# A new plan for the pieces of work behind an expert's twelve weight blocks

## The chip, the cores and the metric

The kernel runs on one core of a Trainium2 chip. The metric is the device time of one execution in microseconds (us), read as the median of several runs. A measurement of this kernel can tell a difference of about 0.2% (some 4 us) from no change.

## The reference, cut to what matters

One layer: a token mixer (which the change does not touch), then a mixture of experts over 1024 tokens of width 1024, a residual add and a last norm. The part that matters, per token block of an expert:

```python
logits = (xt @ w_router + b_router)
top_vals, top_idx = lax.top_k(logits, 4)            # 4 of 32 experts
weights = jax.nn.softmax(top_vals, axis=-1)
...
def expert_block(args):
    xblk, e = args
    gu = xblk @ w_gu[e] + b_gu[e]                    # 1024 -> 2048
    gate, up = jnp.split(gu, 2, axis=-1)
    gate = jnp.minimum(gate, 7.0); up = jnp.clip(up, -7.0, 7.0)
    act = (up + 1.0) * gate * jax.nn.sigmoid(1.702 * gate)
    return act @ w_down[e] + b_down[e]               # 1024 -> 1024
...
y = zeros.at[buf_tok].add(yb * buf_w[:, None])       # rows back to their tokens
```

## The kernel before, in words

**Experts and blocks.** The experts are sorted by how many tokens they have and run in a written-out order, `HHHLLH`, then twelve times `LH`, then `LL` (line 1344). Every expert takes 128 tokens in a main group; a heavy one (H) has one further group of 32 tokens, called the remainder, and the first expert has two. An expert's weights come in twelve blocks of 1 MB, each [128, 2048] in fp32: eight of `w_gu` and four of `w_down`. The loop at line 1770 runs one iteration per expert e: the eight `w_gu` blocks of expert e (`gu_chunk`, blocks 0 to 7), then the four `w_down` blocks of expert e-1 (`dn_chunk`, blocks 8 to 11). With them the activation of expert e (`act`) is put out at block 8, and the weighted rows of e-1 are scattered at the end (`finish_e`). The first iteration has eight blocks only.

**A block.** The matrix products are made exact by splitting each fp32 operand into a high and a low part: ScalarE (ACT) copies the block into the high part, VectorE (DVE) subtracts it to get the low part (`split`, lines 130 to 134), and TensorE (PE) then runs twelve matmuls of 512 columns for the block. The split blocks stand in three buffers `hl`, so ACT can split a block as soon as PE has used the one three places before. For a remainder PE runs further matmuls (`pR`) straight from the fp32 blocks, after blocks 3, 7 and 11. The weights lie in eight slots and are loaded up to five blocks ahead, in order, on the queue of SP.

**The pieces.** Between two blocks `extras(k)` puts out small pieces of work that the next experts need; `plan(e)` (line 1736) is the hand-written list of which piece stands behind which block k. They are:
- `prep_a(e, 0)` and `prep_a(e, 1)`: PE transposes half of the activated rows of expert e into PSUM (`pps`, four transposes), ACT copies the high part, DVE subtracts the low part. `prep_a(e, 2)` does the remainder rows (`ppr`, two transposes): a copy by ACT and no VectorE part.
- `prep_x(e, 0)`, `(e, 1)`, `(e, 2)`: the same for the gathered input rows.
- `prep_sel(e)`: a one-hot table by DVE. `prep_route(e)`: PE multiplies it with a table of indices and weights (`pq`), DVE forms row indices from the result, and GpSimd (POOL) starts the indirect DMAs that gather the rows (`xg`, and `xq` for a remainder).
- In the first two iterations also `bias_rows` (bias tables, four of them), `route_weights` (a transpose `px`, a copy `wT` by ACT, a matmul `pyw`, then five steps that alternate between ACT and DVE), `weigh` (the weights of the first two experts), and `route_counts` and `route_rows` (tables for an overflow path).

**What sets the order.** All of these pieces write one and the same PSUM bank, the single buffer of `ptr` with the tag "t". PE's instructions keep the order of the program (`T.strict`), so PE stands still if a piece comes up while the bank still holds the piece before, that is until ACT and DVE have read it. On ACT and DVE the instructions go through one queue each, in an order that the scheduler of the framework fixes at build time, mostly by which is ready first. POOL's queue holds the gathers and the scatter-adds into `acc` of `finish_e`, where the scatter of remainder rows (`yq`) waits until the scatter of the main rows (`y`) has landed.

Of the kernel before, what the change touches and what calls it, by code (L numbers as in the profile page):

```python
# [9 lines left out]
F32 = mybir.dt.float32  # L10
# [9 lines left out]
P = 128  # L20
# [6 lines left out]
NE = 32  # L27
# [25 lines left out]
def tile_hybrid_layer(ctx: ExitStack, tc: tile.TileContext, x, c, ctx_in, c_ctx, w_ada, b_ada, norm_mix_w,  # L53
# [35 lines left out]
    def pool(name, **kw):  # L89
        return tc.tile_pool(name=name, bufs=kw.pop("bufs", 1), reuse_waits="tile", **kw)  # L90
# [89 lines left out]
    tp = inp.enter_context(pool("tp", bufs=2))  # L180
# [287 lines left out]
    at = [kp.tile([P, 2, 2, P], F32, name=f"at{d}") for d in range(2)]  # L468
# [356 lines left out]
    pb = inp.enter_context(pool("pb"))  # L825
# [74 lines left out]
    lg = rp.tile([P, NT, NE], F32, name="lg")  # L900
# [285 lines left out]
    pdn = mps.enter_context(pool("pdn", space=PSUM))  # L1186
    prm = mps.enter_context(pool("prm", space=PSUM))
    ptr = mps.enter_context(pool("ptr", space=PSUM))
    tp = ms.enter_context(pool("tp3"))
# [33 lines left out]
    for i, v in enumerate((0, 5)):  # L1223
        S.activation(info[:, :, :, v], tcol[:, i, :, None].to_broadcast([P, NT, NE]), AF.Copy)
        S.activation(info[:, :, :, v + 1], pcols[:, i:i + 1, None].to_broadcast([P, NT, NE]), AF.Copy)

    def route_weights():

        flat = lg.rearrange("p t e -> p (t e)")
        S.activation(lgn, lg, AF.Copy)  # L1230
        G.tensor_tensor(bdg, bdg, g2b[0:96], op=ALU.mult)
        px = ptr.tile([P, 2, P], F32, name="px", tag="t")
        for h in range(2):
            T.transpose(px[:, h], flat[:, h * P:(h + 1) * P], ident)
        wT = tp.tile([P, 2, P], F32, name="wT")
        S.activation(wT, px, AF.Copy)
        py = ptr.tile([P, 2, P], F32, name="pyw", tag="t")
        for h in range(2):
            T.matmul(py[:, h], wT[:, h], pbd.rearrange("p j e -> p (j e)"), start=True, stop=True)
        V.tensor_copy(flat, py.rearrange("p h r -> p (h r)"))  # L1240
        eq = tp.tile([P, NT, NE], F32, name="eq")
        S.activation(info[:, :, :, 2], lg, AF.Copy)
        V.tensor_tensor(eq, lg, info[:, :, :, 2], op=ALU.subtract)
        S.activation(info[:, :, :, 3], eq, AF.Copy)
        V.tensor_tensor(eq, eq, info[:, :, :, 3], op=ALU.subtract)
        S.activation(info[:, :, :, 4], eq, AF.Copy)
        for j in range(4):
            S.activation(g2r[32 * j:32 * j + 32], g2b[32 * j:32 * j + 32, 256 * j:256 * j + 256], AF.Copy)

    B = {}  # L1250

    def route_blocks():

        erb = B["erb"] = tp.tile([NE, 2 * NE + 1], F32, name="erb")
        V.tensor_copy(erb[:, 0:NE], pe_[:NE, 0:NE])

    def route_counts():
# [6 lines left out]
        for j in range(7):  # L1264
            dst = nb if j == 0 else tmp1
            V.tensor_scalar(dst, over, float(P * j), None, op0=ALU.is_gt)
            if j:
                V.tensor_tensor(nb, nb, tmp1, op=ALU.add)
        nbb = B["nbb"] = tp.tile([NE, 2, MAXBLK], F32, name="nbb")
        V.tensor_copy(nbb[:, 0], nb.to_broadcast([NE, MAXBLK]))  # L1270
        V.tensor_copy(nbb[:, 1], capc.to_broadcast([NE, MAXBLK]))

    def route_rows():

        nbb, erb = B["nbb"], B["erb"]
        pb = ptr.tile([P, 3, NE], F32, name="pblk", tag="t")
# [45 lines left out]
    def bias_perm():  # L1322
        perm = ap.tile([P, 2 * D], BF16, name="perm", tag="y")[:, 0:1536].rearrange(
            "p (a q n j i) -> p a q n j i", a=3, q=4, n=4, j=8)
        V.memset(perm, 0.0)
        for i in range(3):
            V.tensor_copy(perm[:, i, :, :, :, i], pbd.rearrange("p n (q j) -> p q n j", q=4))
        return perm

    def bias_rows(perm, q):  # L1330
        pb = ptr.tile([P, 512], F32, name="pbq", tag="t")
        for i in range(3):
            T.matmul(pb, perm[:, i, q].rearrange("p n j i -> p (n j i)"), bt[:, i], start=(i == 0), stop=(i == 2))
        S.activation(bq[:, q], pb, AF.Copy)
# [26 lines left out]
    def route_main(i, pq, main):  # L1361

        r, sel = order[i], R["sel", i]
        for t in range(NT):
            T.matmul(pq[:, 0, main], sel[:, t, 0:P], info[:, t, r, main], start=(t == 0), stop=(t == NT - 1))

    def route_rem(i, pq, rem):

        r, sel = order[i], R["sel", i]
        for g in range(nrem[i]):  # L1370
            for t in range(NT):
                for j in range(4):
                    T.matmul(pq[32 * j:32 * j + 32, 1 + g, rem], sel[:, t, P + CAPR * g:P + CAPR * (g + 1)],
                             info[:, t, r, rem], start=(t == 0), stop=(t == NT - 1))
# [27 lines left out]
    def slot_weights(i, pq):  # L1402
        n = 1 + nrem[i]
        wc = xp.tile([P, 3], F32, name="wc", tag="wc", bufs=4)
        V.tensor_reduce(wc[:, :n], pq[:, :n, 2:5], axis=mybir.AxisListType.X, op=ALU.add)  # L1405
        R["wc", i] = wc
# [85 lines left out]
            HL[key] = hl  # L1492
            pos_split[0] += 1

    GU, DN = {}, {}

    def gu_start(e):
        g = pgu.tile([P, 4, 512], F32, name="pG", tag="g")
        rs = []
        if nrem[e]:  # L1500
            rs.append(prm.tile([P, 512], F32, name="pR", tag="r"))
        if nrem[e] > 1:
            rs.append(pdn.tile([P, 2, 512], F32, name="pR1", tag="d")[:, 0])
        GU[e] = (g, rs)

    def gu_bias(e):
# [198 lines left out]
    with tc.high_priority():  # L1705
        for i in range(2):
            if i == 0:
                prep_sel(0, (slice(0, P), slice(P, P + CAPR * nrem[0])))
            pq = ptr.tile([P, 3, 8], F32, name="pq", tag="t")
# [4 lines left out]
            pq = pdn.tile([P, 3, 8], F32, name="pqr", tag="d")  # L1714
# [11 lines left out]
            prep_x(0, p_)  # L1726
    perm = bias_perm()

    def weigh(i):
        pq = ptr.tile([P, 3, 8], F32, name="pq", tag="t")  # L1730
        route_main(i, pq, slice(2, 5))
        route_rem(i, pq, slice(2, 5))
        slot_weights(i, pq)


    def plan(e):
        todo = {}

        def at(k, f, *a):
            todo.setdefault(k, []).append((f, a))  # L1740
        if e == 0:
            for k, q in ((0, 0), (2, 2), (4, 1)):
                at(k, bias_rows, perm, q)
            at(1, route_weights)
            at(3, prep_x, 1, 2)
            at(5, weigh, 0)
            at(5, weigh, 1)
            at(6, prep_x, 1, 0)
            at(7, prep_x, 1, 1)
            at(7, prep_sel, 2)  # L1750
            return todo
        if e == NE:
            return todo
        for k, p in ((0, 0), (2, 1), (4, 2)):
            at(k, prep_a, e - 1, p)
        if e + 1 < NE:
            for k, p in ((5, 0), (7, 1), (9, 2)):
                at(k, prep_x, e + 1, p)
        if e == 1:
            at(1, prep_route, 2)  # L1760
            at(3, route_counts)
            at(6, route_rows)
            at(11, bias_rows, perm, 3)
        if e + 2 < NE:
            at(8, prep_sel, e + 2)
            at(10, prep_route, e + 2)
        return todo

    T.strict = True
    for e in range(nexp + 1):  # L1770
        todo = plan(e)

        def extras(k):
            for f, a in todo.pop(k, ()):
                f(*a)
        if e < nexp:
            gu_start(e)
            for k in range(KT):
                advance()
                gu_chunk(e, k)  # L1780
                extras(k)
# [28 lines left out]
    with ExitStack() as st:  # L1810
# [3 lines left out]
        pdn = st.enter_context(tc.tile_pool(name="pdn2", bufs=1, space=PSUM, reuse_waits="tile"))  # L1814
        ptr = st.enter_context(tc.tile_pool(name="ptr2", bufs=1, space=PSUM, reuse_waits="tile"))
        again = nc.values_load(nblk1[0:1, 1:2], min_val=0, max_val=1)  # L1816
        with tc.For_i(0, again, 1):
# [5 lines left out]
            with tc.For_i(0, nblk, 1) as ib:  # L1823
# [27 lines left out]
                pq = ptr.tile([P, 8], F32, name="opq", tag="t")  # L1851
                for t in range(NT):
                    T.matmul(pq[:, 0:4], sel[:, t], oi[:, t, 0:4], start=(t == 0), stop=(t == NT - 1))
                q = op.tile([P, 8], F32, name="oq")
# [33 lines left out]
                g = op.tile([P, D], F32, name="og_")  # L1888
# [19 lines left out]
            for t in range(NT):  # L1908
                rs_ = slice(t * P, (t + 1) * P)
                h = op.tile([P, D], F32, name="oh", tag="oh", bufs=2)  # L1910
# [12 lines left out]
                rs = op.tile([P, 1], F32, name="or", tag="or", bufs=2)  # L1923
# [31 lines left out]
```

## Time and profile before

| | us |
|---|---|
| median of 3 runs (lowest, highest) | 1967.25 (1966.44, 1969.1) |
| the profiled execution's own time | 1970.1 |
| its span, first to last instruction | 1968.0 |
| TensorE busy in it | 1865.0 |
| VectorE busy | 1542.4 |
| ScalarE busy | 1134.6 |

The last three overlap each other; a busy time says how full an engine's own queue was and not what the kernel waits for. The mixer takes the first 538 us of the span, the experts 538 to 1935, the last norm the rest.

### The profile page before, as it was taken

How to read it: one execution, taken by the hardware profiler on the slowest of the kernel's cores; microseconds unless marked ns; L12 is line 12 of the kernel's file. 1: busy time of each engine (PE TensorE's matmuls, PEld its weight loads, DVE VectorE, ACT ScalarE, POOL GpSimd, SP SyncE). 2: the span in 40 equal slices, each digit the busy share in tenths (PEclk: the TensorE clock that was granted, in tenths of full speed). 3: DMA queues.
4: the chain of work that ended last, by engine and by line, in shares of the span. 5: the costliest groups of instructions: out<-in, count | busy, mean ns of one | idle time of the engine just before them, and what ended most of it. 6: DMA issues, size and time to landing. Idle time of an engine off the chain costs nothing. (4 is left out here: it accounts for less than half of the span.)

```text
span 1968.0 us, 29495 instructions
## 1 busy us (share of the span) xinstructions
PE 1865.0 (95%) x11470; PEld 1373.3 (70%) x11473; DVE 1542.4 (78%) x1608; ACT 1134.6 (58%) x1265; POOL 341.9 (17%) x236
## 2 busy tenths in 40 slices
PE   6999997999598999999999999999999999999996
PEld 3777675777456677777677777767777676777764
DVE  4476479558766789889898888989888898887887
ACT  3554556644444566656565666656666565656663
POOL 2010033010400113111112111113111112221012
PEclk9999998999698999999999999999999999999998
DMA  9284522214555789889789898978889798898985
GB/s 346 86 300 142 170 97 98 89 53 186 204 212 226 262 314 379 321 306 366 272 327 347 314 346 304 366 273 331 342 299 363 273 364 307 326 337 303 367 321 183
DMA packets 125528, 532.33 MB, mean 270 GB/s; under 512 B 13196, under 2 KB 27328, under 8 KB 90568
## 3 DMA queue, kind: packets, MB, share of 16 engines
q1 hardware_dynamic: 109464, 481.82, 62.6%
q0 software_dynamic: 15344, 48.01, 9.3%
q8 instruction: 92, 1.51, 0.3%
q10 hardware_dynamic: 576, 0.56, 0.1%
q14 instruction: 52, 0.43, 0.1%
HBM read 497.68 MB, written 32.67 MB: 269 GB/s over the span
## 5 line engine op out<-in xcount | busy, mean ns | idle before, releaser
L74 PE MATMUL pG<-hl,xT 128*128 128x512 f32 x3072 | 766.9, 403 | 0.0
L74 PEld LDWEIGHTS pG<-hl,xT 128*128 128x128 f32 x3072 | 570.3, 190 | 147.6 <-issue 21.5
L132 DVE TENSOR_TENSOR hl<-ring,hl 128x2048 fp32r<-128x2048 f32 (+2 forms) x199 | 397.9, 2006 | 162.9 <-ACT hl L131 162.2
L131 ACT ACTIVATE hl<-ring 128x2048 fp32r<-128x2048 f32 (+2 forms) x199 | 331.4, 1667 | 282.4 <-PE pG L74 160.2
L132 DVE TENSOR_TENSOR hl<-mix,hl 128x2048 fp32r<-128x2048 f32 x144 | 329.4, 2289 | 82.8 <-ACT hl L131 82.8
L131 ACT ACTIVATE hl<-mix 128x2048 fp32r<-128x2048 f32 (+1 forms) x146 | 277.7, 1903 | 183.5 <-PE pG L74 145.4
L74 PE MATMUL pD<-hl,aT 128*128 128x512 f32 x1488 | 367.7, 401 | 1.1 <-DVE hl L132 1.1
L74 PEld LDWEIGHTS pD<-hl,aT 128*128 128x128 f32 x1488 | 274.3, 188 | 63.6 <-DVE hl L132 2.2
L131 ACT ACTIVATE hl<-ringx 128x2048 fp32r<-128x2048 f32 x96 | 184.3, 1920 | 97.4 <-PE pG L74 57.7
L132 DVE TENSOR_TENSOR hl<-ringx,hl 128x2048 fp32r<-128x2048 f32 x96 | 219.5, 2287 | 26.4 <-ACT hl L131 25.3
L1384 POOL DMA_INDIRECT xg<-h2d,ix x32 | 73.3, 2290 | 886.9 <-DVE wc L1405 848.6
L74 PE MATMUL pa<-hl,hi 128*128 128x512 f32 x544 | 180.1, 417 | 5.7 <-DVE wsg L760 3.5
L74 PEld LDWEIGHTS pa<-hl,hi 128*128 128x128 f32 x544 | 102.4, 197 | 31.4 <-DVE wsg L760 4.8
L1598 POOL DMA_INDIRECT acc<-y,ix x31 | 104.9, 3383 | 87.2 <-DVE y L1593 87.2
L74 PE MATMUL pa<-hl,lo 128*128 128x512 f32 x272 | 107.6, 407 | 0.0
L74 PE MATMUL pa<-hi,hl 128*128 128x512 f32 (+1 forms) x288 | 95.2, 393 | 1.0 <-ACT hi L400 1.0
L74 PEld LDWEIGHTS pa<-hi,hl 128*128 128x128 f32 x288 | 54.7, 192 | 16.3 <-issue 3.1
L1603 POOL DMA_INDIRECT acc<-yq,ixr x17 | 34.5, 2031 | 169.7 <-DVE hl L132 70.6
L1544 ACT ACTIVATE ag<-ag 128x1024 f32<-128x1024 f32 (+1 forms) x49 | 41.0, 836 | 39.4 <-DVE ag L1543 39.4
L74 PEld LDWEIGHTS pa<-hl,lo 128*128 128x128 f32 x272 | 52.5, 195 | 11.9 <-issue 1.1
L74 PE MATMUL pa<-lo,hl 128*128 128x512 f32 (+1 forms) x144 | 55.0, 385 | 1.8 <-DVE lo L401 1.8
L74 PE MATMUL pR<-ring,xqT 128*32 128x512 f32 x408 | 53.3, 596 | 0.0
(390 smaller groups left out, 2012.0 us busy)
## 6 DMA issues: line engine op xcount, KB each, us to landing
ring<-in_w_gu_dram SPq DMA_DIRECT2D x96, 1024.0 KB, 14.3
mix<-in_w_gu_dram SPq DMA_DIRECT2D x96, 1024.0 KB, 10.1
ringx<-in_w_gu_dram SPq DMA_DIRECT2D x64, 1024.0 KB, 7.2
ring<-in_w_down_dram SPq DMA_DIRECT2D x48, 1024.0 KB, 7.8
mix<-in_w_down_dram SPq DMA_DIRECT2D x48, 1024.0 KB, 14.6
ringx<-in_w_down_dram SPq DMA_DIRECT2D x32, 1024.0 KB, 15.8
ring<-in_w_in_dram SPq DMA_DIRECT2D x32, 512.0 KB, 6.4
ring<-in_w_ada_dram SPq DMA_DIRECT2D x16, 1024.0 KB, 6.0
```

The costliest lines, as they stand in the source:

```text
L74: i = nc.tensor.matmul(*a, **k)
L131: S.activation(hl[:, 0], src, AF.Copy)
L132: i = eng.tensor_tensor(hl[:, 1], src, hl[:, 0].bitcast(F32), op=ALU.subtract)
L1384: nc.gpsimd.indirect_dma_start(out=xg, out_offset=None, in_=h2d, in_offset=bass.IndirectOffsetOnAxis(ap=ix[:, 0:1], axis=0))
L1544: pin(S.activation(g, g, AF.Gelu_apprx_sigmoid))
L1598: nc.gpsimd.indirect_dma_start(out=acc, out_offset=bass.IndirectOffsetOnAxis(ap=ix[:, 0:1], axis=0), in_=y, in_offset=None, compute_op=ALU ...
L1603: nc.gpsimd.indirect_dma_start(out=acc4, out_offset=bass.IndirectOffsetOnAxis(ap=ixr[g][:, 0:1], axis=0), in_=yq, in_offset=None, compute_ ...
```

## The change

The plan gets new places, and the first expert gets a second bank. In its iteration the second half of the two-bank PSUM tile `pR1`, whose first half takes the first expert's second remainder, is unused; it is handed out as `SPARE[0]`.

In the first iteration three of the four `bias_rows` and the transpose `px` use the spare bank. `route_weights` is cut in two, so that the matmul `pyw` that needs the copy `wT` comes one block later. Both `weigh` become one piece in the spare bank that runs the matmuls of both experts and then the two reductions. The remainder piece `prep_x(1, 2)` goes to block 0 of the second iteration, and the last `bias_rows` comes from there into the first.

From the second iteration on the places are:

| piece | before | after |
|---|---|---|
| `prep_a(e-1)`, parts 0, 1, 2 | 0, 2, 4 | 3, 5, 7 |
| `prep_x(e+1)`, parts 0, 1, 2 | 5, 7, 9 | 9, 11, 8 |
| `prep_sel(e+2)` | 8 | 6 |
| `prep_route` | 10, for e+2 | 1, for e+1 |
| `route_counts`, `route_rows` | 3 and 6 of e = 1 | 7 of e = 7, 7 of e = 9 |

```diff
     def route_weights():
         flat = lg.rearrange("p t e -> p (t e)")
         S.activation(lgn, lg, AF.Copy)
         G.tensor_tensor(bdg, bdg, g2b[0:96], op=ALU.mult)
-        px = ptr.tile([P, 2, P], F32, name="px", tag="t")
+        px = SPARE[0][:, 0:2 * P].rearrange("p (h t) -> p h t", h=2)
         for h in range(2):
             T.transpose(px[:, h], flat[:, h * P:(h + 1) * P], ident)
-        wT = tp.tile([P, 2, P], F32, name="wT")
+        wT = B["wT"] = tp.tile([P, 2, P], F32, name="wT")
         S.activation(wT, px, AF.Copy)
+
+    def route_weights2():
+        flat = lg.rearrange("p t e -> p (t e)")
+        wT = B["wT"]
         py = ptr.tile([P, 2, P], F32, name="pyw", tag="t")
...
     def bias_rows(perm, q):
-        pb = ptr.tile([P, 512], F32, name="pbq", tag="t")
+        pb = SPARE[0] if q else ptr.tile([P, 512], F32, name="pbq", tag="t")
...
         if nrem[e] > 1:
-            rs.append(pdn.tile([P, 2, 512], F32, name="pR1", tag="d")[:, 0])
+            r1 = pdn.tile([P, 2, 512], F32, name="pR1", tag="d")
+            rs.append(r1[:, 0])
+            SPARE[0] = r1[:, 1]
...
-    def weigh(i):
-        pq = ptr.tile([P, 3, 8], F32, name="pq", tag="t")
-        route_main(i, pq, slice(2, 5))
-        route_rem(i, pq, slice(2, 5))
-        slot_weights(i, pq)
+    def weigh():
+
+        pq = SPARE[0][:, 0:48].rearrange("p (i g v) -> p i g v", i=2, g=3)
+        for i in range(2):
+            route_main(i, pq[:, i], slice(2, 5))
+            route_rem(i, pq[:, i], slice(2, 5))
+        for i in range(2):
+            slot_weights(i, pq[:, i])
...
         if e == 0:
-            for k, q in ((0, 0), (2, 2), (4, 1)):
+            for k, q in ((0, 0), (0, 1), (3, 2), (4, 3)):
                 at(k, bias_rows, perm, q)
             at(1, route_weights)
-            at(3, prep_x, 1, 2)
-            at(5, weigh, 0)
-            at(5, weigh, 1)
-            at(6, prep_x, 1, 0)
-            at(7, prep_x, 1, 1)
+            at(2, route_weights2)
+            for k, p in ((4, 0), (6, 1)):
+                at(k, prep_x, 1, p)
+            at(6, weigh)
             at(7, prep_sel, 2)
             return todo
         if e == NE:
             return todo
-        for k, p in ((0, 0), (2, 1), (4, 2)):
+        if e == 1:
+            at(0, prep_x, 1, 2)
+        if e + 1 < NE:
+            at(1, prep_route, e + 1)
+        for k, p in ((3, 0), (5, 1), (7, 2)):
             at(k, prep_a, e - 1, p)
+        if e == 7:
+            at(7, route_counts)
+        if e == 9:
+            at(7, route_rows)
         if e + 1 < NE:
-            for k, p in ((5, 0), (7, 1), (9, 2)):
+            for k, p in ((8, 2), (9, 0), (11, 1)):
                 at(k, prep_x, e + 1, p)
-        if e == 1:
-            at(1, prep_route, 2)
-            at(3, route_counts)
-            at(6, route_rows)
-            at(11, bias_rows, perm, 3)
         if e + 2 < NE:
-            at(8, prep_sel, e + 2)
-            at(10, prep_route, e + 2)
+            at(6, prep_sel, e + 2)
         return todo
```

## Rows read from the trace of the kernel before

**Rows 1.** The page, busy time of each engine.

```profile
PE 1865.0 (95%) x11470; PEld 1373.3 (70%) x11473; DVE 1542.4 (78%) x1608; ACT 1134.6 (58%) x1265; POOL 341.9 (17%) x236
```

**Rows 2.** A stretch: length, busy PE, PEld, DVE, ACT, POOL; granted clock, DMA share, GB/s.

```profile
587.60:651.40 63.80, 58.30 (x430) 39.76 (x430) 44.22 (x69) 28.32 (x23) 4.83 (x3) 0.92 0.58 218
```

**Rows 3.** PE's waits, 540 to 655, then 655 to 1900: total, times, longest.

```profile
PE pyw L74 <- ACT wT L1236: 2.1, 1, 2.1
PE ppr L79 <- ACT aqT L1429: 2.1, 1, 2.1
PE pblk L74 <- DVE xT L1423: 1.7, 1, 1.7
PE pq L74 <- DVE aT L1423: 1.7, 1, 1.7
PE pq L74 <- DVE wc L1405: 0.3, 1, 0.3
...
PE ppr L79 <- DVE xT L1423: 7.3, 13, 0.6
PE pD L74 <- DVE hl L132: 1.1, 2, 0.9
```

**Rows 4.** Stretches around the half clock, columns as in Rows 2.

```profile
549.10:552.50 3.40, 3.34 (x10) 2.86 (x11) 2.39 (x2) 0.98 (x2) 0.00 (x0) 0.51 0.86 357
597.00:600.30 3.30, 3.30 (x9) 2.57 (x8) 2.62 (x5) 0.00 (x0) 1.74 (x1) 0.50 0.02 7
627.80:1917.00 1289.20, 1277.26 (x7778) 935.85 (x7777) 1093.95 (x779) 800.67 (x558) 229.30 (x89) 1.00 0.86 324
```

**Rows 5.** Timeline, second iteration: start, length, engine, line, operation, [idle before <-releaser].

```profile
590.49 0.60 PE L79 MATMUL pps<-ident,at 128*128 128x128 f32 x4
590.85 3.04 PE L74 MATMUL pG<-hl,xT 128*128 128x512 f32 x12
592.51 0.58 ACT L1422 ACTIVATE aT<-pps 128x512 fp32r<-128x512 f32 x1
594.85 0.68 DVE L1423 TENSOR_TENSOR aT<-pps,aT 128x512 fp32r<-128x512 f32 x1
595.58 0.63 PE L74 MATMUL pq<-info,sel 128*128 128x5 bf16 x40 [1.70 <-DVE aT L1423]
596.14 4.61 PE L74 MATMUL pG<-hl,xT 128*128 128x512 f32 x12
```

**Rows 6.** Timeline before the experts: the second of two remainder transposes.

```profile
538.44 0.69 PE L79 MATMUL ppr<-ident,xq 128*128 128x128 f32 x2 [1.08 <-ACT xqT L1429]
```

**Rows 7.** Timeline of a light expert, from the end of its block 7.

```profile
1016.42 0.60 PE L79 MATMUL pps<-ident,xg 128*128 128x128 f32 x4
1016.62 1.92 ACT L131 ACTIVATE hl<-ringx 128x2048 fp32r<-128x2048 f32 x1 [0.88 <-PE pG L74]
1018.44 0.57 ACT L1422 ACTIVATE xT<-pps 128x512 fp32r<-128x512 f32 x1
1019.23 1.06 ACT L1544 ACTIVATE ag<-ag 128x1024 f32<-128x1024 f32 x1 [0.21 <-DVE ag L1543]
1020.19 1.90 ACT L131 ACTIVATE hl<-ring 128x2048 fp32r<-128x2048 f32 x1
1022.44 0.68 DVE L1423 TENSOR_TENSOR xT<-pps,xT 128x512 fp32r<-128x512 f32 x1
1023.18 0.44 PE L79 MATMUL ppr<-ident,xq 128*128 128x128 f32 x2 [0.56 <-DVE xT L1423]
1024.18 4.48 DVE L132 TENSOR_TENSOR hl<-ring,hl 128x2048 fp32r<-128x2048 f32 x2
```

**Rows 8.** Third iteration: the last scatter, a gather's landing, PE at block 8.

```profile
673.28 3.38 POOL L1603 DMA_INDIRECT acc<-yq,ixr  x1 [6.93 <-DMA acc<-yq,ixr]
...
DMA to landing us min/median/max: 5.3/9.9/11.7
...
683.91 8.65 PE L74 MATMUL pD<-hl,aT 128*128 128x512 f32 x36
```

More of the change, by code (lines that the diff above doesn't have):

```diff
@@ L1225, in tile_hybrid_layer @@
         S.activation(info[:, :, :, v + 1], pcols[:, i:i + 1, None].to_broadcast([P, NT, NE]), AF.Copy)
+    B = {}
     def route_weights():
@@ L1248, in route_weights @@
             S.activation(g2r[32 * j:32 * j + 32], g2b[32 * j:32 * j + 32, 256 * j:256 * j + 256], AF.Copy)
-    B = {}
     def route_blocks():
@@ L1493, in split_to @@
             pos_split[0] += 1
-    GU, DN = {}, {}
+    GU, DN, SPARE = {}, {}, [None]
     def gu_start(e):
```

## The prediction

> **What bounds it now.** First the busy times of the page [rows 1]: TensorE is busy 95% of the span, VectorE 78%. A busy time doesn't name a bound, so the span is cut into stretches next. From the third iteration nearly to the end (the last line of [rows 4]) TensorE is busy in 1277.26 of 1289.2 us at the full clock: the experts are bound by TensorE, and only the 12 us in which it stands still can be won there without taking work away (8.4 of them are waits that the list below names). The second iteration [rows 2] is the loose one: 5.5 of its 63.8 us idle and a mean clock of 0.92. The list of TensorE's own waits says what it stood still for [rows 3]: up to 655 us five waits of 7.9 us in all (2.1, 2.1, 1.7, 1.7 and 0.3), later 13 equal ones of 0.56 us before `ppr` (7.3 us) and two for a split block (1.1 us).
>
> The timeline shows how such a wait comes about [rows 5]. The transposes `pps` end at 591.1 and TensorE goes on with a block of 3.04 us. ACT, which begins a split the moment a block ends, copies `pps` at 592.51 only; VectorE, likewise with a split first, subtracts at 594.85 and is done at 595.5. Till then the bank is taken. The next piece, `pq`, stands one block behind and so waits 1.70 us. A piece with a VectorE part thus holds the bank for about 4.4 us, longer than the block of 3.04 us that follows it: two such pieces must not stand behind neighbouring blocks. And the block behind this wait takes 4.61 us: the clock granted there is 0.50, 1.2 in place of 2.4 GHz [rows 4]. There are four such half-clock stretches of 3.4 us, each beginning where one of the four waits of 1.7 us and more ends. Behind the thirteen waits of 0.56 us there is none: 1.00 all the way to 1917.
>
> The 13 later waits are all in light experts whose successor is heavy [rows 7]. The half `pps` behind block 7 is copied by ACT at 1018.44, but VectorE subtracts at 1022.44, because the activation of the expert and a split stand before it; the `ppr` behind block 9 waits for that until 1023.18.
>
> **The change, part by part.** All prices are from the profiled execution of 1970.1 us (span 1968.0). It is 2.85 us above the median of 1967.25, so I take the saving off the median.
>
> *Waits of the first two iterations.* In the first, `pyw` comes a block later than the transpose it needs, and one block (3.04 us) covers the copy `wT`: the 2.1 us go. One `weigh` with one wait less: 0.3 go. In the second, no piece with a VectorE part stands behind a neighbour any more (places 1, 3, 5, 9, 11; 0, 7 and 8 have a copy by ACT alone), so both waits of 1.7 go. The wait of 2.1 for `aqT` lies between the two `ppr` of the first expert; that pair moves from block 4 to block 7, where it comes behind the remainder's matmuls. It can't fall below the copy that lies between them (an estimate: 0.4 us, some two thirds of the 0.57 that the copy of a half of twice its size takes [rows 7]), and it stays at 2.1 if ACT is in a split again. The nearest row is the other pair, 1.08 us [rows 6], with a split before the copy; behind the remainder the split should be over, so I take 0.6. Won: 7.9 - 0.6 = 7.3 us; ends 5.8 and 7.5. The remainder piece of the second expert, now behind block 0, meets only `pq` behind block 1 and is freed by a copy of ACT within the block between them.
>
> *The clock.* If the four long waits go, so do the four stretches: each 3.4 us at half speed is 1.7 us lost, together 6.8 us. Ends 0 (they come whatever the waits) and 6.8; I take 6.8, because all four begin at the end of such a wait.
>
> *The 13 waits.* The half that VectorE frees late goes to blocks 9 and 11. Behind 7 and 8 stand two `ppr`, which ACT alone frees. Along [rows 7]: `ppr` at 1016.42, ACT's split until 1018.44, the copy (some 0.4) in the place of the 0.57, then the activation's ACT part at 1019.23, done by 1020.19. The second `ppr` comes one block after the first, about 1019.4, to a free bank. ACT then has a split from 1020.19 to 1022.1 and the second copy to about 1022.4, and the `pps` behind block 9 comes up at about 1022.45: hardly any room. I allow 0.1 us for each of the 12 light experts with two heavy neighbours: 7.3 - 1.2 = 6.1 us won; ends 0 (a wait of 0.56 again) and 7.3.
>
> *VectorE beside the activation.* Without the 0.68 us at 1022.44 the two splits of 1024.18 come 0.6 us earlier. The fourth of the `w_down` blocks needs the first of them, which is done at 1026.4, just before TensorE gets there (1023.18 + 0.2 + 3.04). TensorE will come 0.5 us earlier, so this stays as tight as it is. Of the 1.1 us of waits `pD` I count 0.6 as won.
>
> *Gathers, moved past the scatters.* `prep_route` goes from behind block 10 to behind block 1 of the next iteration, so on POOL's queue its gather now stands behind the scatters of `finish_e`, of which the `yq` wait for the landing of `y`. The worst place is the third iteration, with two `yq` before it, the last running until 676.7 [rows 8]; a gather behind it lands 9.9 us after its issue, at most 11.7, that is by 686.9 to 688.7. It is needed behind block 9, at 683.91 + 2/3 of 8.65 = 689.7: it is in time by 1 to 3 us. Elsewhere at most one `yq` stands before it. Cost 0; with this cover gone, 2 us once. The weights' loads stay as they are: SP's queue has nothing new to pass.
>
> *What only moves.* `prep_sel`, `bias_rows`, `route_counts` and `route_rows` do the same work in other places; TensorE's part of them costs the same. VectorE's steps of the last two now meet an activation, once each, in iterations 7 and 9, both heavy, where TensorE has the remainder's matmuls to go on with. Cost 0, or one wait of 0.56 to 2.1 each.
>
> **Sum.** 7.3 + 6.8 + 6.1 + 0.6 = 20.8 us; 1967.25 - 20.8 = 1946.5 us, 1.1% less.
>
> **Rivals.**
>
> *The opening alone.* The margin behind blocks 7 to 9 is not there, because ACT takes a split before the copy once more, and the thirteen waits come back at another place. For it: a margin below 0.1 us. Against it: ACT's order in [rows 7] puts the copy first. Time: 1946.5 + 6.1 = 1952.6. Chance 0.18.
>
> *The half-clock stretches stay.* They begin at the waits, but in the same place there is also a run of transposes and tiny matmuls, which stay. Then the waits go and the clock falls all the same: 1946.5 + 6.8 = 1953.3. The Trainium skill (TensorE: Matmul & The Clock Gate, "Why this matters for your kernels") speaks for this rival: it asks only that idle gaps longer than any of these four be avoided, so by it they would not be what brings the half clock. By that rule the time would be 1953.3, and by the rows 1946.5; the trace is against the rule so far, with four stretches behind four waits. Chance 0.08.
>
> *Slower: the copy behind the activation on ACT.* Blocks 7 and 8 now both need the bank, and ACT's order is fixed at build time. If at 1018.44 the activation's part (ready at 1019.2, 1.06 us) goes before the copy, the bank comes free at 1020.65 in place of 1018.8, and the second `ppr`, due at 1019.4, waits 1.2 us, in 12 light experts. That alone is 14.4 us and gives 1960.9. If 1.2 us is also enough for the half clock (0.56 was not, 1.70 was), each costs 1.7 more: 12 x 2.9 = 34.8, and 1946.5 + 34.8 = 1981.3. It decides from 20.8 / 12 = 1.7 us an expert. Against it: in [rows 7] ACT copies before it activates, and the copy is ready 2.4 us earlier. Chance 0.07.
>
> *It doesn't do what it says.* The scheduler puts VectorE's and ACT's steps in another order, so that the opening's pieces hold the bank as long as before and only some waits go: 1960 to 1967. Chance 0.07.
>
> **How the numbers follow.** That leaves 0.60 for the forecast, 1946.5, with its own range of 1942 to 1950: down by the waits left in the sum (0.2 + 1.2 + 0.5) and the runs' spread of 1 to 2 us, up by a long wait in the pair of `ppr` with its half clock (3.2 us). The first two rivals lie at 1953, and with the spread of the runs the range must reach 1957 to hold them. 1941 to 1957 leaves out the last two rivals and little else. About 4 us (0.2%) is what a measurement of this kernel can tell from no change. Everything but the slower rival and the upper part of the last is faster by more than that: 0.88 faster, 0.05 the same, 0.07 slower.
>
> **What would show it.** In the waits of TensorE: no `pyw`, `pq` or `pblk` before 655; one `ppr` on `aqT` of about 0.6; none of the 13 on `xT`. In the granted clock: 1.00 from about 540 to the last expert. In the timeline of a light expert: `aqT` copied before `ag`, and the `pps` behind block 9 within 0.2 us of the block's end. I am wrong if a stretch of half clock stands where no wait is, if `pps` waits on a copy by ACT in every light expert, or if a transpose waits for a gather's landing.

## The result, and the profile after

The changed kernel takes 1946.40 us (median of 4 runs, 1946.22 to 1946.77) against 1967.89 us for the kernel before on the same chip (4 runs, 1966.44 to 1969.1). The ratio is 0.9894, with a 95% interval of 0.9882 to 0.9906: 21.5 us less, where 20.8 less had been forecast. The profiled execution of the changed kernel took 1946.54 us, its span 1944.7.

TensorE runs as many matmuls as before, and its busy time fell by 8.6 us (1865.0 in [rows 1]) where the span fell by 23.3. So 14.7 us came from where it stood still, and the rest from where it ran slowly. The page of the changed kernel:

```profile
PE 1856.4 (95%) x11471; PEld 1371.6 (71%) x11473; DVE 1541.2 (79%) x1608; ACT 1134.2 (58%) x1265; POOL 341.0 (18%) x236
```

The span of the changed kernel, cut at the first block of an expert's iteration: first iteration, second, third to 31st, then the last expert and the norm. Columns as in [rows 2]. The two lines behind them are the first iteration and the third to 31st of the kernel before.

```profile
537.17:581.37 44.20, 43.99 (x382) 27.04 (x382) 29.85 (x22) 25.33 (x21) 0.00 (x0) 0.97 0.56 226
581.37:634.13 52.76, 52.28 (x416) 35.83 (x413) 39.54 (x34) 28.17 (x23) 7.21 (x3) 1.00 0.65 256
634.13:1859.27 1225.14, 1222.21 (x7440) 900.21 (x7438) 1051.17 (x771) 766.57 (x535) 220.16 (x87) 1.00 0.86 327
1859.27:1944.70 85.43, 62.17 (x271) 49.14 (x269) 65.57 (x48) 41.81 (x41) 19.75 (x21) 0.87 0.70 261
...
538.78:587.62 48.84, 46.31 (x382) 28.38 (x382) 30.69 (x23) 24.86 (x21) 0.00 (x0) 0.93 0.53 211
651.43:1883.87 1232.44, 1224.06 (x7421) 897.76 (x7420) 1047.48 (x736) 767.80 (x536) 222.50 (x87) 1.00 0.86 324
```

| stage | before | after | difference |
|---|---|---|---|
| to the first expert block | 538.78 | 537.17 | -1.6 |
| first iteration | 48.84 | 44.20 | -4.6 |
| second iteration | 63.81 | 52.76 | -11.0 |
| third to 31st | 1232.44 | 1225.14 | -7.3 |
| last expert and norm | 84.13 | 85.43 | +1.3 |

The first and the last line are not the change's. The code ahead of the experts is the same, and over all the runs below the first expert block starts at 534.9 to 539.7. At the end both kernels have a wait of 3.8 us in the last expert, with a half clock behind it that lasted 6.8 us here and 3.4 us in the trace of before. The second iteration, with a mean clock of 0.92 in [rows 2], now runs at 1.00 and with 0.5 us of idle time.

TensorE's waits after, from 538 to 655 and from 640 to 1900 (total, times, longest), to be held against [rows 3]:

```profile
PE ppr L79 <- ACT aqT L1433: 0.5, 1, 0.5
PE pR L74 <- issue: 0.2, 1, 0.2
...
PE pps L79 <- DVE at L1552: 3.8, 1, 3.8
PE pps L79 <- ACT xqT L1433: 2.7, 12, 0.2
PE pps L79 <- DVE xT L1427: 0.3, 1, 0.3
```

All five waits of the opening are gone but for 0.47 us in the pair of `ppr`; one of 0.16 us, which waits for nothing that the profile shows, is new. The 13 waits on `xT` and the two on `hl` (8.4 us) are gone too, and 2.9 us stand in their place: twelve of 0.22, where `pps` waits for the copy `xqT`, and one of 0.28. (The 3.8 is the last expert's, as before.) A light expert in the timeline shows where the 0.22 comes from, with the same columns as [rows 7]:

```profile
996.84 0.38 PE L79 MATMUL ppr<-ident,at 128*128 128x128 f32 x2
998.86 0.36 ACT L1433 ACTIVATE aqT<-ppr 128x256 f32<-128x256 f32 x1
999.86 0.38 PE L79 MATMUL ppr<-ident,xq 128*128 128x128 f32 x2
1000.06 1.92 ACT L131 ACTIVATE hl<-ring 128x2048 fp32r<-128x2048 f32 x1 [0.83 <-PE pD L74]
1001.88 1.04 ACT L1550 ACTIVATE ag<-ag 128x1024 f32<-128x1024 f32 x1
1002.83 0.36 ACT L1433 ACTIVATE xqT<-ppr 128x256 f32<-128x256 f32 x1
1003.25 0.66 PE L79 MATMUL pps<-ident,xg 128*128 128x128 f32 x4 [0.22 <-ACT xqT L1433]
```

ACT makes the first copy ahead of the activation, so the second `ppr` meets a free bank. The second copy then stands behind a split and the activation, and is done at 1003.19, just after `pps` comes up at 1003.03.

### The profile page after: what moved, and what is told of

It is laid out like the page before. It is cut to its first block, busy times and chain, and to the rows that moved or that the text cites. A ratio compares the mean times of both kernels' runs of the same rounds, so it can differ in the third digit from the quotient of the medians.

```text
span 1944.7 us, 29489 instructions
## 1 busy us (share of the span) xinstructions
PE 1856.4 (95%) x11471; PEld 1371.6 (71%) x11473; DVE 1541.2 (79%) x1608; ACT 1134.2 (58%) x1265; POOL 341.0 (18%) x236
## 5 line engine op out<-in xcount | busy, mean ns | idle before, releaser
L74 PE MATMUL pG<-hl,xT 128*128 128x512 f32 x3072 | 750.1, 399 | 0.0
L1426 ACT ACTIVATE xT<-pps 128x512 fp32r<-128x512 f32 x64 | 37.3, 583 | 44.7 <-PE pps L79 41.5
L1426 ACT ACTIVATE aT<-pps 128x512 fp32r<-128x512 f32 x62 | 36.0, 581 | 41.9 <-PE pps L79 41.9
L1427 DVE TENSOR_TENSOR aT<-pps,aT 128x512 fp32r<-128x512 f32 x62 | 42.5, 685 | 16.5 <-ACT aT L1426 16.5
## 6 DMA issues: line engine op xcount, KB each, us to landing
mix<-in_w_gu_dram SPq DMA_DIRECT2D x96, 1024.0 KB, 13.6
```

What stands on the lines that cost most here:

```text
L74: i = nc.tensor.matmul(*a, **k)
L1426: S.activation(dst[:, 0, part], pp, AF.Copy)
L1427: V.tensor_tensor(dst[:, 1, part], pp, dst[:, 0, part].bitcast(F32), op=ALU.subtract)
```

## The experiments

**The two halves of the plan.** *The new opening alone:* the first two iterations as in the changed kernel, the old places from the fourth on; the third is a transition, with its `prep_route` in a bank of its own, and the two overflow tables stand behind block 11 of e = 7 and 9.

```diff
+        if e == 2:
+            at(0, prep_a, 1, 0)
+            at(1, prep_route, 3, True)
...
+        if e > 2:
+            for k, p in ((0, 0), (2, 1), (4, 2)):
+                at(k, prep_a, e - 1, p)
...
```

> The new first two iterations, then (with one iteration of transition, whose routing uses a bank of its own) the old places for the pieces. Theory (what is saved is TensorE's waits for the bank and the half clock that follows each wait of 1.7 us or more, place by place, so the two halves of the change add up): the opening's 14 to 15 us come, the 13 waits of 0.56 us stay; 1968 - 14.5 = 1953.5 us, 1952 to 1956; granted clock 1.00 from the first experts to the last. Rival A (the later places are worth nothing, all came from the opening): 1946 to 1948. Rival B (the opening is worth its waits of 7 us alone, the half clock comes from elsewhere): 1961.

Measured: 1954.48 us against 1967.84 (ratio 0.9935, 0.9918 to 0.9952), 13.4 us less. The first two iterations take 44.77 and 52.76 us, with no half clock behind the first block; the transition and the tables cost 1.8 us later. Its waits from 640 to 1960 are those of [rows 3], unchanged:

```profile
PE ppr L79 <- DVE xT L1430: 7.4, 13, 0.6
...
PE pD L74 <- DVE hl L132: 1.1, 2, 0.9
```

*The new places from the third iteration alone*, the opening as before:

```diff
+        if e > 1:
+            if 2 < e < NE - 1:
+                at(1, prep_route, e + 1)
+            for k, p in ((3, 0), (5, 1), (7, 2)):
+                at(k, prep_a, e - 1, p)
+            if e + 1 < NE:
+                for k, p in ((8, 2), (9, 0), (11, 1)):
+                    at(k, prep_x, e + 1, p)
...
```

> The old first two iterations with one bank, the new places from the third iteration on (the overflow tables stay in the second iteration). Theory: 7.3 us as between the two traces (1232.4 against 1225.1 from the third iteration to the last), so 1968 - 7 = 1961 us, 1959.5 to 1962.5; the five long waits and the four half-clock stretches of the opening stay; the 13 waits of 0.56 become 12 of 0.22. Rival A (the later places are worth nothing): 1967 to 1968.

Measured: 1960.21 us (ratio 0.9969, 0.995 to 0.9987), 7.6 us less. Its waits, 537 to 655, then 655 to 1900:

```profile
PE pyw L74 <- ACT wT L1236: 2.3, 1, 2.3
PE ppr L79 <- ACT aqT L1429: 2.1, 1, 2.1
PE pblk L74 <- DVE xT L1423: 1.7, 1, 1.7
PE pq L74 <- DVE aT L1423: 1.7, 1, 1.7
...
PE pps L79 <- ACT xqT L1429: 2.6, 12, 0.2
```

The halves add up within their intervals: 13.4 + 7.6 = 21.0 us against 21.5 for the whole. The gain in the later iterations is real, so the rival "the opening alone" falls. But this profile also held a surprise: four long waits stand in the opening as before, and only one stretch of half clock, behind the last of them.

**Waits or pieces?** *The kernel before, every piece in its old place, but in the second iteration `pq`, the second `ppr` of the first expert and `pblk` in another PSUM bank*, so that the waits go and the runs of small matmuls stay.

```diff
-        pb = ptr.tile([P, 3, NE], F32, name="pblk", tag="t")
+        pb = BK[0][:, 0, 0:3 * NE].rearrange("p (g v) -> p g v", g=3)
...
-        pq = ptr.tile([P, 3, 8], F32, name="pq", tag="t")
+        if i == 2:
+            BK.append(pdn.tile([P, 2, 512], F32, name="pbk", tag="d"))
+            pq = BK[0][:, 0, 0:24].rearrange("p (g v) -> p g v", g=3)
...
```

> The kernel before with every piece in its old place; in the second iteration alone three pieces (pq, the second ppr of the first expert, pblk) write another PSUM bank. Nothing moves and the number of transposes is the same, only the waits for the bank go. Theory: the three waits of 1.70, 2.05 and 1.70 us go and with them the three half-clock stretches of the second iteration: 1968 - 10.5 = 1957.5 us, 1956.5 to 1959; granted clock 0.50 near 549 only. Rival (the half clock comes from the run of transposes and tiny matmuls and not from the waits): the waits go, the three stretches stay, 1968 - 5.4 = 1962.5 us.

Measured: 1958.59 us (ratio 0.996, 0.9946 to 0.9975), 9.3 us less by the bank alone. The three waits of the second iteration (2.1, 1.7, 1.7) are gone and so is every slow stretch in it (the seventh number of the stretch is the clock):

```profile
586.00:650.00 64.00, 63.95 (x479) 44.95 (x479) 50.24 (x73) 34.98 (x28) 12.11 (x4) 1.00 0.71 256
```

Only the one behind `pyw`, in the first iteration, is left. The second iteration takes 53.33 us where it took 63.81: 10.48 less, 5.5 of it the waits, which leaves 1.66 us for each of three stretches. The half clock goes with the waits while the pieces stay, which speaks against that rival. This is one execution; the whole set of traces settles it. From 545 us to the last expert's wait no stretch of half clock stands in any of the fourteen traces without a wait of TensorE of 1.70 us or more at it, and the pieces stand in all of them.

**Does every such wait bring the half clock?** *The kernel before, twice more, nothing edited.*

> The kernel before once more, for its clock alone. Theory now (after a run in which the same four waits of the opening brought one half-clock stretch only, and one in which 6 of 15 waits of 1.75 to 2.15 us brought one): a wait of about 2 us brings the half clock in some executions and not in others, so the number of stretches between 545 and 650 us differs from the four of the first trace, and the time differs by 1.7 us for each: 1964 (none) to 1970 (four). Rival: four stretches every time, and 1970.

> The kernel before a third time, with the same expectation: fewer than four stretches, or another set of waits that bring them, and a time that goes with their number at 1.7 us each; by the rival four stretches and 1970 us.

Measured: 1965.18 and 1966.07 us. Both have the same four waits as [rows 3] (the first of them 2.25 and 2.36 us long here), and only one half-clock stretch, behind the last. From the first of the two, the timeline:

```profile
593.74 0.63 PE L74 MATMUL pq<-info,sel 128*128 128x5 bf16 x40 [1.70 <-DVE aT L1423]
594.31 3.06 PE L74 MATMUL pG<-hl,xT 128*128 128x512 f32 x12
610.15 0.44 PE L79 MATMUL ppr<-ident,at 128*128 128x128 f32 x2 [2.05 <-ACT aqT L1429]
610.34 3.04 PE L74 MATMUL pG<-hl,xT 128*128 128x512 f32 x12
618.31 0.24 PE L74 MATMUL pblk<-linc,nbb 32*32 32x32 f32 x2 [1.71 <-DVE xT L1423]
618.61 4.57 PE L74 MATMUL pG<-hl,xT 128*128 128x512 f32 x12
```

and two stretches:

```profile
585.80:619.50 33.70, 28.24 (x199) 20.05 (x197) 22.34 (x35) 16.50 (x14) 2.83 (x2) 1.00 0.66 254
619.90:623.10 3.20, 3.20 (x8) 1.98 (x6) 1.66 (x6) 0.00 (x0) 0.00 (x0) 0.50 0.00 0
```

The block behind `pq` takes 3.06 us, where in [rows 5] it took 4.61 behind the same wait of 1.70. So the wait is needed for the half clock and doesn't always bring it. The second iteration, 63.81 us with three stretches, is 60.67 and 60.70 with one: some 1.56 us for each of the two that are missing. The first of these runs started its experts at 538.82, as the profiled run of before did, and took 4.9 us less: three stretches.

**Beside and behind the activation.** *The changed kernel with the halves of `prep_x` behind blocks 8 and 9, neighbours, the first of them beside the activation.*

```diff
-            for k, p in ((8, 2), (9, 0), (11, 1)):
+            for k, p in ((8, 0), (9, 1), (11, 2)):
```

> The changed kernel with the two halves of the input transposes behind blocks 8 and 9 and the remainder's behind 11: VectorE parts beside the activation and behind neighbouring blocks again. Theory: the half behind 8 is freed only when VectorE has done the activation and two splits, some 7 to 10 us after block 7 ends, and the half behind 9 is due after 6 us: a wait of 1 to 4 us in each of the 15 light experts from the third on, less in the heavy ones; with the half clock (1.7 us) behind each wait of 1.7 us and more, 15 x (2.5 + 1.7) = 63 us slower, 1980 to 2030 us. Rival (VectorE beside the activation is not what counts): up to 15 x 0.56 = 8 us, 1946 to 1956.

Measured: 2070.66 us in a single run, above all that had been expected (1980 to 2030): heavy experts wait as well. TensorE's waits from 690 to 1990:

```profile
PE pps L79 <- DVE xT L1427: 80.8, 27, 3.9
```

Two of them in the timeline, in a light and in a heavy expert:

```profile
1045.62 1.11 PE L79 MATMUL pps<-ident,xg 128*128 128x128 f32 x4 [3.68 <-DVE xT L1427]
...
1096.84 0.66 PE L79 MATMUL pps<-ident,xg 128*128 128x128 f32 x4 [2.10 <-DVE xT L1427]
```

The stretch behind each, the first at half clock and the second not:

```profile
1045.20:1048.40 3.20, 2.78 (x9) 2.40 (x10) 3.17 (x3) 0.60 (x1) 0.00 (x0) 0.50 0.00 0
1097.00:1100.20 3.20, 3.20 (x17) 2.65 (x17) 2.66 (x2) 0.60 (x1) 0.00 (x0) 1.00 1.02 428
```

This run serves as a scale for the clock. All 15 waits of 3.68 to 3.90 us among the pieces were followed by a half clock, and 6 of the 15 of 1.75 to 2.15.

*Two blocks apart, but still beside the activation:* halves behind 8 and 10, and part 2 behind block 0 of the iteration that uses it. The edit is against the last version below, which has the halves behind 9 and 11; in the fifth iteration, the only one where part 2 had stayed behind block 8, it goes behind block 11.

```diff
-                at(8, prep_x, e + 1, 2)
+                at(11, prep_x, e + 1, 2)
-            for k, p in ((9, 0), (11, 1)):
+            for k, p in ((8, 0), (10, 1)):
```

> That version with the two halves of the input behind blocks 8 and 10: a VectorE part beside the activation, but no neighbour within two blocks. Theory A (only the bank counts: a piece may stand beside the activation if the next use of the bank is two blocks away): the half behind 8 holds the bank 6 us, the next is due after 5.7: a wait of 0.2 to 0.4 us in each light expert, 1942.6 + 15 x 0.3 = 1947, 1945 to 1949. Theory B (the part also delays the splits behind it on VectorE by 0.68 us, and the last blocks of w_down come to wait for their split as they did in two places before, 0.88 us at most): 0.5 to 0.9 us more in each of the 15 light experts, 1953 to 1960, with the waits at pD on a split.

Measured: 1960.68 us (ratio 0.9968, 0.9955 to 0.998), against 1945.6 for the version with the halves behind 9 and 11: 15.1 us lost, where theory A had 2.4 to 6.4 and theory B 10.4 to 17.4, counted from the 1942.6 that both start at. 2.6 of it are the fifth iteration's, where the moved part 2 waits 1.56 us as well. Fifteen light experts wait, 13.6 us in all, in the list of waits from 655 to 1890:

```profile
PE pps L79 <- DVE xT L1427: 13.6, 15, 1.1
PE ppr L79 <- DVE xT L1427: 1.6, 1, 1.6
```

One of them in the timeline:

```profile
1003.52 0.60 PE L79 MATMUL pps<-ident,xg 128*128 128x128 f32 x4
1006.49 0.57 ACT L1426 ACTIVATE xT<-pps 128x512 fp32r<-128x512 f32 x1
1008.72 1.22 DVE L1552 SCALAR_TENSOR_TENSOR at<-at,ag 128x1024 f32<-128x1024 f32 x1
1009.85 0.69 DVE L1427 TENSOR_TENSOR xT<-pps,xT 128x512 fp32r<-128x512 f32 x1
1010.60 0.66 PE L79 MATMUL pps<-ident,xg 128*128 128x128 f32 x4 [0.88 <-DVE xT L1427]
```

The place is the one of theory A, the piece two blocks on, and the size the one of theory B, 0.88 us; no wait at `pD` stands in the list. From the first transpose at 1003.52 to 1010.54 the half holds the bank for 7.0 us, where the one of [rows 5], away from the activation, holds it for 5.0 (590.49 to 595.53; the 4.4 of the prediction count from the end of the transposes): ACT's copy stands behind a split and the activation, and VectorE's part behind two splits and the last step of the activation. The next piece is due at 1009.72, 6.2 us after the first: two blocks cover 5.0 us and not 7.0. None of these waits brought a half clock.

**The second bank.** *The changed kernel, with its opening pieces in the one shared bank again.*

```diff
-        px = SPARE[0][:, 0:2 * P].rearrange("p (h t) -> p h t", h=2)
+        px = ptr.tile([P, 2, P], F32, name="px", tag="t")
...
-        pb = SPARE[0] if q else ptr.tile([P, 512], F32, name="pbq", tag="t")
+        pb = ptr.tile([P, 512], F32, name="pbq", tag="t")
...
-        pq = SPARE[0][:, 0:48].rearrange("p (i g v) -> p i g v", i=2, g=3)
+        pq = ptr.tile([P, 2, 3, 8], F32, name="pq", tag="t")
```

> The changed kernel without the spare bank: the first expert's tables are at their new places but all in the one bank. Theory: each pair of pieces behind one block now waits for ACT's copy of the first, which comes after a split (2.1 to 2.5 us: two bias tables behind block 0, a bias table and a half of the input behind block 4), and the weights' piece behind block 6 waits for VectorE's part of the half (4.4 us): about 9 us of waits, and up to three half-clock stretches of 1.7 us: 1946.4 + 9 to 14 = 1955 to 1960.5 us. Rival (the places alone matter, the bank doesn't): 1946 to 1948.

Measured: 1959.29 us (ratio 0.9949, 0.9933 to 0.9965). The first iteration takes 54.78 us where the changed kernel's takes 44.20. The waits from 537 to 640:

```profile
PE pq L74 <- DVE xT L1427: 4.5, 1, 4.5
PE pps L79 <- ACT bq L1338: 1.9, 1, 1.9
PE pbq L74 <- ACT bq L1338: 1.8, 1, 1.8
```

The stretch at the longest, which ends at 578.80:

```profile
577.20:584.10 6.90, 5.30 (x121) 4.49 (x121) 4.32 (x6) 0.00 (x0) 0.00 (x0) 0.51 0.01 2
```

8.2 us of waits come, with one stretch twice as long as the others at the 4.5; behind the two short waits there is none. In this dense first iteration the plan depends on the second bank.

**A version with more room.** The 0.22 us arises because the light expert's second `ppr` stands one block ahead of `pps`. *The changed kernel with part 2 of `prep_x` always behind block 0 of its own iteration:*

```diff
-        if e == 1:
-            at(0, prep_x, 1, 2)
+        at(0, prep_x, e, 2)
...
-            for k, p in ((8, 2), (9, 0), (11, 1)):
+            for k, p in ((9, 0), (11, 1)):
```

> The changed kernel with one more move: the remainder piece of the input, prep_x(e+1, 2), goes from behind block 8 to behind block 0 of its own expert's iteration, as the second expert already has it. Theory (the 12 waits of 0.22 us are TensorE behind ACT's copy of that piece, which comes after a split and the activation): they go and nothing takes their place, 1946.4 - 2.7 = 1943.7 us. Rival (the piece then comes one block behind the half that VectorE frees late at the end of the iteration, or delays the routing piece behind block 1): a wait of 0.5 us or more in each light or heavy expert takes their place, 1946 to 1960.

Measured: 1946.65 us (ratio 0.9888, 0.9872 to 0.9905), no gain that shows. A pair of a light and a heavy iteration did fall, from 84.70 to 84.38 us, but in the sixth iteration, the one heavy expert that follows a light one which itself follows a light one, `ppr` comes up 2.7 us before VectorE has freed the bank, and the half clock follows: 48.37 us in place of 43.74. Between block 11 of the iteration ahead and block 0 there are no remainder matmuls here to give cover.

*The same, and where the expert of two iterations earlier has no remainder, the piece stays behind block 8:*

```diff
-        if e == 1:
-            at(0, prep_x, 1, 2)
+        if e == 1 or nrem[e - 2]:
+            at(0, prep_x, e, 2)
...
-            for k, p in ((8, 2), (9, 0), (11, 1)):
+            if not nrem[e - 1]:
+                at(8, prep_x, e + 1, 2)
+            for k, p in ((9, 0), (11, 1)):
```

> As the version with the remainder piece of the input behind block 0 of its own expert's iteration, but only where remainder matmuls of 4 us stand between it and the half freed late (12 of the 14 places); in the fifth iteration, where they don't and the piece waited 2.7 us with a half-clock stretch behind it, it stays behind block 8 of the iteration before. Theory: the 12 light-heavy pairs come in 84.4 in place of 84.7 us as in that version, and the sixth expert's iteration in 43.7 again in place of 48.4: 1946.4 - 3.8 = 1942.6 us. Rival (what the pairs won was given back elsewhere): 1946.

Measured: 1945.6 us (ratio 0.9885, 0.9868 to 0.9901), by the median nearer to the rival. From the first expert's first block to the last's it takes 1319.0 us, the changed kernel 1322.1. To settle so little, the changed kernel and this one ran once more, on one chip:

> The changed kernel again, on one chip with the version below. 1946.4 us as before; no half-clock stretch between the first expert and the last.

> The version with the remainder piece behind block 0 of its own iteration (behind block 8 for the sixth expert) again, beside the changed kernel on one chip. Theory: from the first expert's first block to the last expert's it takes 3.1 us less (1319.0 against 1322.1 in the two traces), and the two medians differ by about that, 2 to 4 us; the 0.8 us between the medians of different chips was the start of the experts, which lies anywhere from 534.9 to 539.7 us. Rival: on one chip they agree within 1 us.

Measured: 1947.73 us (1944.96 to 1948.34) for the changed kernel, ratio 0.9903 (0.9886 to 0.992), and 1943.81 (1941.95 to 1945.6) for the new version, ratio 0.9891 (0.9875 to 0.9908). The new version is 3.9 us below the changed one on the same chip, 3.1 us by its trace, and has the lower median in both of its runs. It is the version that beats both, but its lead over the changed kernel is at the limit of what is measurable: the two intervals overlap. Neither profiled execution has a half clock between the first expert's second block and the last expert.

## Why the prediction was right, step by step

**The waits of the first two iterations: right.** 7.9 us fell to 0.47 (forecast: 0.6). The pieces with a VectorE part no longer stand behind neighbours, and the pair of `ppr` keeps the least that the copy costs.

**The clock: the cause was right and the size was that of one execution.** The step said that all four stretches begin at the end of such a wait (0.01 to 1.37 us behind it, in the trace), and valued them at 6.8 us. For the profiled execution that holds: 3 x 1.66 us in the second iteration and about as much in the first. But the same waits bring four stretches in one run and one in three others. What the step should have priced was a chance per wait, not four certain stretches. In an execution with four stretches the clock's part is 4 x 1.66 = 6.6 us, in one with one 1.7 us. How many there are in a median run of the kernel before no run here shows. Of the runs without a trace there is only the mean clock of the whole execution, and the mixer and the end have half-clock stretches of their own. It points the same way: of 34 executions of the kernel before, the six fastest (1963.06 to 1964.88 us) have a mean clock of 0.976 to 0.980, the six slowest (1969.5 to 1972.68) one of 0.974 to 0.976. The rival in which the stretches stay is refuted all the same: without the waits none is left in the opening. The rule cited with that rival (the Trainium skill, TensorE: Matmul & The Clock Gate, "Why this matters for your kernels") asks only that longer gaps be avoided, and so by itself would have waits of this length bring no half clock. The traces differ: of the waits of 1.70 to 2.36 us in the runs above 14 of 34 were followed by one.

**The 13 waits: gone, and a term was missing.** ACT put `aqT` ahead of `ag` as read from [rows 7], so the slower rival didn't happen. But a split that the forecast had behind `ag` came between the two, and the second copy, which it had end just before `pps` comes up, ends 0.16 us after. So the wait left over is 12 x 0.22 and not 12 x 0.1. One of the prediction's signs of being wrong, `pps` waiting on a copy by ACT, came true in these twelve light experts: the order behind `aqT` came out otherwise than forecast, and it cost 1.4 us. Both waits at `pD` went (1.1 us, forecast 0.6). That makes 8.4 - 2.9 = 5.5 us, where the two steps together had 6.7. Yet the stage won 7.3, and it took in the two tables (0.46 us) and the `prep_route` of the fourth expert from the second iteration. The 2.5 us beyond the waits (7.3 + 0.46 + 0.22 for that `pq` - 5.5) aren't in TensorE's list. They are spread thinly: a light and a heavy iteration together went from 85.13 to 84.70 us, 0.09 more than the 0.34 of the wait. In the sixth iteration, which has no wait in either kernel, it went from 44.38 to 43.74, and only 0.37 of that is its `pq`, now the smaller one of a light expert (0.22 us in place of 0.59 in the stream of matmuls). In the new plan `pq` stands together with the bias behind block 1 and some pieces behind the remainder's matmuls, so the stream of blocks is cut at fewer places: seven uncut runs of blocks became six in a heavy iteration, nine became seven in a light one. The thirtieth iteration, heavy, with the same `pq` and no wait in either kernel, went from 43.74 to 43.66. But a light iteration stayed at 41.0 though its wait shrank by 0.34 and only its `pq` grew, by 0.37, so there the two cuts less bring nothing that shows. The step "what only moves" had counted such places at nothing. That the fewer cuts are the cause is argued from these lengths and not shown; most of the 2.5 us stays open.

**The gathers: the cost was right, the order wrong.** The step had the gather of the third iteration stand behind both scatters of `yq`, with 1 to 3 us to spare. POOL's queue after in the timeline, and TensorE's first use of the rows:

```profile
643.93 2.77 POOL L1609 DMA_INDIRECT acc<-yq,ixr  x1 [10.74 <-DMA acc<-y,ix]
647.00 1.33 POOL L1388 DMA_INDIRECT xg<-h2d,ix  x1 [0.30 <-issue]
649.16 2.45 POOL L1609 DMA_INDIRECT acc<-yq,ixr  x1 [0.83 <-DMA acc<-yq,ixr]
...
671.57 0.60 PE L79 MATMUL pps<-ident,xg 128*128 128x128 f32 x4
```

The gather went between the two scatters, at 647.00, and TensorE wants its rows at 671.57. With the slowest landing of this kernel's gathers, 13.3 us, that still leaves more than 10 us. In the iterations after it the gather even goes ahead of the `yq`: the queue's order is not that of the plan.

**What only moves.** `route_counts` and `route_rows` add 0.15 and 0.31 us to the iterations of e = 7 and 9 (43.80 and 43.96 us, against 43.65 for their like) and no wait.

**The sum** came to within 0.1 us of the median, which is luck. It took prices from an execution with four stretches, 2.85 us above the median, off the median. The clock term is too large for some runs of the kernel before by up to 5 us, the terms of the later iterations too small by 0.6 us, and the first iteration gained 0.6 us beyond its waits and its stretch (4.64 against 2.05, 0.3 and 1.66), most of it because its first block ran slower in the trace of before (4.65 us against 4.14): the half clock from before the experts lasted 3.5 us into it, against 2.4. The median was also carried by a run-to-run spread that nothing in the sum stands for: over all comparisons here the kernel before lay between 1963.06 and 1972.68 us.

## What to carry to other kernels

Where small pieces of work share one PSUM buffer, measure from the timeline how long each holds it, from its first transpose to the end of the last engine that reads it, and place them so that the next is due later than that: here 5.0 us away from the activation and 7.0 beside it, against 3.4 to the next piece one block on and 6.2 two blocks on. A second bank for a crowded stretch does the same without moving anything (9.3 us here). Price a clock stretch seen in one trace as a chance, and look at a second profile of the same kernel before adding it to a sum.

## What the runs showed of the hardware that was not expected

The half clock behind a short wait is a matter of the execution. Among the experts the granted clock stayed at 1.00 after all waits of TensorE of up to 0.90 us, and after the two single ones of 1.11 and 1.56. After waits of 1.70 to 2.36 us it fell to 0.5, that is 1.2 in place of 2.4 GHz, in 14 of 34 cases, the very same wait of the same kernel in one run and not in another, and each fall cost some 1.55 to 1.9 us (by the second iteration: 63.81 us with three, 60.70 with one, 53.33 with neither waits nor falls). After the one wait of 2.74 us it fell, after those of 3.68 to 3.90 us in all 15 cases, and at the 3.8 us of the last expert in all fourteen traces; such a fall lasts 3.4 or 6.8 us, as does the one at the wait of 4.54 us (6.8).

The last norm has a wait of 1.59 us in all fourteen traces. In twelve the clock stays at 1.00 behind it, in two it falls 1.6 us later. One of the two, and the same place in the changed kernel:

```profile
1913.66 1.17 PE L74 MATMUL pF<-wb 96*128 96x512 f32 x4 [1.59 <-ACT yhl L131]
1914.66 3.08 PE L74 MATMUL pF<-yhl,to 128*128 128x512 f32 x8
...
1915.49 1.17 PE L74 MATMUL pF<-wb 96*128 96x512 f32 x4 [1.59 <-ACT yhl L131]
1916.49 2.03 PE L74 MATMUL pF<-yhl,to 128*128 128x512 f32 x8
```

What decides between the two outcomes of a wait of 2 us no run here shows. The falls may also be behind much of the spread of the times, which is argued and not shown: the kernel before, with four such waits, moved over 9.6 us in all its executions here, the changed kernel, with none of them in the opening and far fewer executions, over 3.4 (1944.96 to 1948.34).
